# Decays of the SSD scan kept as exponentials in DRAM, with the cumulative sums and the long conv moved

## The chip, the cores and the metric

One core of a Trainium2 chip runs the whole program. The metric is the device time of one execution in microseconds. The core's engines run side by side, each from its own in-order queue: TensorE (PE, matrix products), VectorE (DVE), ScalarE (ACT), GpSimd (POOL) and SyncE (SP). They wait for one another by semaphores. DMAs are issued from the queues of SP, ACT and POOL.

## The reference, cut to what matters

One layer of a decoder trunk for 2048 prompt tokens and 8 x 8 sample tokens. After an RMS norm, one projection feeds three mixers (a Mamba-2 scan "SSD", a Conformer convolution, causal pooling), whose outputs are projected, gated and added.

```python
def trunk(x, states, start_pos, params):
    h = rmsnorm(x, norm_w)
    z, xbc, dt_raw, glu_in, gate_b, u_pool, gate_c, merge = split(h @ w_in)
    ya = mamba_branch(z, xbc, dt_raw, ...)     # conv of 4 taps, SSD scan, gated norm
    yb = conformer_branch(glu_in, gate_b, ...) # GLU, conv of 31 taps, layer norm
    yc = pool_branch(u_pool, gate_c, ...)
    ga, gb, gc = split(sigmoid(merge))
    x = x + (ga * (ya @ w_a) + gb * (yb @ w_b) + gc * (yc @ w_c)) @ w_out
    return rmsnorm(x, final_norm_w)

def ssd_scan(x, dt, a_log, b_mat, c_mat, h0):   # chunks of 128 tokens, 16 heads
    a_cum = cumsum(dt * A)                      # inside a chunk
    decay = exp(where(mask, a_cum[l] - a_cum[s], -inf))
    y_diag = (C_l . B_s) * decay @ (x * dt)
    states = B * exp(a_cum[last] - a_cum) * (x * dt)
    h = exp(a_cum[last]) * h + states           # chunk after chunk
    y_off = C * exp(a_cum) * h_enter
    return y_diag + y_off, h
```

## The kernel before, in words

All weights and activations of the large products are split into a high and a low float16 part; a block of a product takes 3 x 8 matmuls of 128 x 128 by up to 512 columns (`mm3`, L355). Tokens come in five blocks of 512, 512, 512, 256 and 320 columns (`TB`; `hT0` to `hT4` are the normed inputs). The order on PE is written by hand for the whole program; the order on DVE is written by hand in two stretches (`order.open()`), elsewhere a scheduler places the instructions of DVE, ACT, POOL and SP when the program is built. Weights come through a loader in steps: load, maximum on ACT (L227), a diagonal (L127), a PE product (L135) whose maximum DVE takes (L137, `prw`), powers of two on POOL (L157 to L241), the high part on ACT (L246), the low part on DVE (L250).

The stages that matter here, in order:

- GLU, second half: for each block four products (two of `glu_g`, two of `glu_v`; column pairs 2 and 3), evicted by a sigmoid on ACT (L446, tile `sg`) and a product on DVE (L455, tile `vt`). The PSUM tiles `mm` have three buffers. Before it, the time steps of the SSD heads are computed on DVE in a chain of small operations that ends with `dtA` (L611). After block 0 comes `cumulate` (L617 ff.): products of `dtA` with triangles and ones on PE (tile `dpt`, three buffers), copies `at` and `acum` and exponentials `etot`, `etos`, `dte` on ACT. The cumulative sums go to DRAM (`acT_d`, `acTs_d`), transposed. After blocks 1 to 3 `decay_early` loads and computes the decays of the first three scan units.
- DVE also runs the 31-tap convolution (`conv31`, L714; pieces of 1024 tokens, one accumulator `acc`, stored by POOL to `c_d`, L732): 68 steps ahead of the xbc stage, 1.9 per 512 columns inside it.
- xbc stage: 12 column blocks of products, evicted by ACT into `ue` (L766), convolved over 4 taps (`ct`, L780, L782), passed through SiLU to DRAM.
- Scan: a unit is a chunk `c` and a head group `g`, 17 x 2 units. Each loads `R` (cumulative sums broadcast over 128 partitions, 8 heads, 512 KB, L656) and `R2` (the same rows, broadcast over 64 partitions for each head of a pair, two DMAs of 128 KB, L662). ACT turns `R` into decays between tokens (8 Relus L672, one exponential L673) and `R2` into exp(a_cum) (L674). DVE forms `xd` (L871), `R` times `cbm` (L873) and, after PE's `off` products, `R2` times `off` (L899) plus `y` (L900); `R2` then leaves for `y_d` on POOL's queue (L903). `R` and `R2` have four buffers each. Between a unit's parts PE does the products of the pooling branch and a gate (`fillers`), at a pace set by `SR`; `pu` (L982) and `sgc` (L1032) are their evictions on ACT, `sw` (L1001) the pooling sums on DVE, `pus` (L987) a load of sample states. In each unit `conv_steps(CB)` is called twice.
- The sample pieces of the long conv (4 of them, 64 tokens) take seven steps each: products `pr` (L728) in four steps, reductions (L730) in two, and one more. The other pieces take 32 steps (31 operations of 512 columns and an empty one). `conv_steps(4)` is called for each of eight sample states at the scan's end, and `conv_steps(7)` for each unit of the merge.
- Merge of the first branch (`merge_units(0)`): gate product, projection, evictions on ACT (L1184) and DVE (L1189). Beside it run the rest of the long conv on DVE and the layer norm `ln_all`, which starts 12 us of the hand order's own clock after the merge does.
- Then the second branch, the gated norm of the scan's output, the third branch and the output product.

Of the kernel before, what the change touches and what calls it, by code (L numbers as in the profile page):

```python
# [10 lines left out]
F32 = mybir.dt.float32  # L11
# [3 lines left out]
AF = mybir.ActivationFunctionType  # L15
ALU = mybir.AluOpType
AX = mybir.AxisListType
# [3 lines left out]
P = 128  # L21
# [3 lines left out]
TS = 64  # L25
NB = 8
AHEAD = 2
TL = 8
T = TP + TS
H = 16  # L30
# [21 lines left out]
def trunk_body(tc, I, O):  # L52
# [16 lines left out]
    drp = pool("dram", 1, space=DRAM)  # L69
# [542 lines left out]
    acT_d = drp.tile([NC * H, P], F32, name="acT_d")  # L612
    acTs_d = drp.tile([H, TS], F32, name="acTs_d")

    def cumulate():

        def dpt(n):  # L617
            return dps.tile([P, 512], F32, name="dpt", tag="dpt", bufs=3)[:, :n]

        for i in range(2):  # L620
            pa = dpt(P)
            PE.matmul(pa, dtA[:, i * P:(i + 1) * P], tri, start=True, stop=True)
            at = tp.tile([P, P], F32, name="at", tag="at", bufs=2)
            S.activation(at, pa, AF.Copy)
            DMA.dma_start(out=acT_d[i * P:(i + 1) * P], in_=at)
        pa = dpt(TS)
        PE.matmul(pa[:H], dtA[:TS, NC * H:ND], tris, start=True, stop=True)
        at = tp.tile([P, P], F32, name="at", tag="at", bufs=2)
        S.activation(at[:H, :TS], pa[:H], AF.Copy)
        DMA.dma_start(out=acTs_d, in_=at[:H, :TS])  # L630
        pa = dpt(ND)
        PE.matmul(pa[:, :NC * H], tri, dtA[:, :NC * H], start=True, stop=True)
        PE.matmul(pa[:TS, NC * H:], tris, dtA[:TS, NC * H:ND], start=True, stop=True)
        S.activation(acum[:, :NC * H], pa[:, :NC * H], AF.Copy)
        S.activation(acum[:TS, NC * H:], pa[:TS, NC * H:], AF.Copy)
        pa = dpt(ND)
        PE.matmul(pa[:, :NC * H], ones, dtA[:, :NC * H], start=True, stop=True)
        PE.matmul(pa[:TS, NC * H:], blks, dtA[:TS, NC * H:ND], start=True, stop=True)
        S.activation(etot, pa[:, :NC * H], AF.Exp)
        V.tensor_tensor(dte[:, :NC * H], pa[:, :NC * H], acum[:, :NC * H], op=SUB)  # L640
        V.tensor_tensor(dte[:TS, NC * H:], pa[:TS, NC * H:], acum[:TS, NC * H:], op=SUB)
        S.activation(dte[:, :NC * H], dte[:, :NC * H], AF.Exp)
        S.activation(dte[:TS, NC * H:], dte[:TS, NC * H:], AF.Exp)

        dtm = tp.tile([P, NB, H], F32, name="dtm")
        V.tensor_tensor(dtm[:TS], dtA[:TS, NC * H:ND].unsqueeze(1).to_broadcast([TS, NB, H]),
                        ind.unsqueeze(2).to_broadcast([TS, NB, H]), op=MUL)
        pa = dpt(NB * H)
        PE.matmul(pa, ones[:TS], dtm[:TS].rearrange("p b h -> p (b h)"), start=True, stop=True)
        S.activation(etos, pa.rearrange("p (b h) -> p b h", h=H), AF.Exp)  # L650

    def decay_load(c, g):
        L = P if c < NC else TS
        R = dcp.tile([P, 8, P], F32, name="R", tag="R")[:, :, :L]
        rows = acT_d[c * H + 8 * g:c * H + 8 * g + 8] if c < NC else acTs_d[8 * g:8 * g + 8]
        DMA.dma_start(out=R[:L], in_=rows.unsqueeze(0).to_broadcast([L, 8, L]))  # L656

        def decays():

            R2 = dcp.tile([P, 4, P], F32, name="R2", tag="R2")[:, :, :L]  # L660
            for hh in range(2):
                DMA.dma_start(out=R2[hh * 64:(hh + 1) * 64],  # L662
                              in_=rows.rearrange("(b two) l -> two b l", two=2)[hh].unsqueeze(0).to_broadcast([64, 4, L]))
            return R2

        return R, decays

    def decay_exp(c, g, L, R, R2):

        for h in range(8):  # L670
            col = c * H + 8 * g + h
            S.activation(R[:L, h], R[:L, h], AF.Relu, scale=-1.0, bias=acum[:L, col:col + 1])  # L672
        S.activation(R[:L], R[:L], AF.Exp, scale=-1.0)  # L673
        S.activation(R2, R2, AF.Exp)  # L674


    early = {}
# [1 line left out]
    def decay_early(c, g):  # L679
        R, decays = decay_load(c, g)  # L680
        early[c, g] = R, decays()
        decay_exp(c, g, P, *early[c, g])

    for bi in range(5):
        for cb in (2, 3):
            glu_v(cb, (bi, 0, TB[bi][1]), wv2, iv2, glu_g(cb, (bi, 0, TB[bi][1]), wg2, ig2))
        if bi == 0:
            cumulate()
        elif bi < 4:
            decay_early(*((0, 0), (0, 1), (1, 0))[bi - 1])  # L690
    dps.release()
    tp.release()
    gp.release()
# [7 lines left out]
    def conv31(cp_, cb, t0, n, bufs):  # L701

        acc = cp_.tile([P, n], F32, name="acc", tag="acc", bufs=1)
        if t0 < TP:
            vt = cp_.tile([P, 30 + n], F32, name="vx", tag="vx", bufs=bufs)
            if t0 == 0:
                G.memset(vt[:, :30], 0.0)
                DMA.dma_start(out=vt[:, 30:], in_=v_d[cb, :, :n])
            else:
                DMA.dma_start(out=vt, in_=v_d[cb, :, t0 - 30:t0 + n])  # L710
            V.tensor_scalar(acc, vt[:, 30:], fw[:, cb, 30:31], fb[:, cb:cb + 1], op0=MUL, op1=ADD)
            for j in range(30):
                yield
                V.scalar_tensor_tensor(acc, vt[:, j:j + n], fw[:, cb, j:j + 1], acc, op0=MUL, op1=ADD)  # L714
        else:
            vt = cp_.tile([P, NB, TL + 30], F32, name="vs", tag="vx", bufs=bufs)
            DMA.dma_start(out=vt[:, :, :30], in_=I["st_cf"][cb])
            DMA.dma_start(out=vt[:, :, 30:], in_=v_d[cb, :, t0:t0 + n].rearrange("p (b t) -> p b t", t=TL))
            DMA.dma_start(out=O["cf_s"][cb], in_=vt[:, :, TL:])
            dst = acc.rearrange("p (b t) -> p b t", t=TL)  # L720
            w_ = fw[:, cb].unsqueeze(1).to_broadcast([P, NB, 31])
            for h in range(0, TL, 4):
                yield
                pr = ssp.tile([P, NB, 4, 31], F32, name="pr", tag="pr", bufs=1)
                for t in range(4):
                    if t == 2:
                        yield
                    V.tensor_tensor(pr[:, :, t], vt[:, :, h + t:h + t + 31], w_, op=MUL)  # L728
                yield
                V.tensor_reduce(dst[:, :, h:h + 4], pr, axis=AX.X, op=ADD)  # L730
            S.activation(acc, acc, AF.Identity, bias=fb[:, cb:cb + 1])
        G.dma_start(out=c_d[cb, :, t0:t0 + n], in_=acc)  # L732
        conv_done.append((cb, t0))
        yield
# [122 lines left out]
    def ssd_front(c, g, L, R, R2, xc):  # L857
# [4 lines left out]
            PE.transpose(px[:L, b * P:(b + 1) * P], xc[:, b], ident)  # L862
            yield
        if (c, g) not in early:
            decay_exp(c, g, L, R, R2)
        gs = slice(c * H + 8 * g, c * H + 8 * g + 8)
        return c, g, L, gs, R, R2, px, cbm

# [187 lines left out]
    fill = fillers()  # L1056
    SR = 1.7
    SI = 8
    CB = 0.3
    CC = 7.0  # L1060
    YP = (2.0, 3.0)
    SA, SC = 1, 4.0
# [190 lines left out]
            yield from ln_steps(bi)  # L1253
            yield LN_GAPS[3]

    side.add(ln_all(), 12.0)
    for _ in merge_units(0):
        conv_steps(CC)
        if not ybp and len(yc16) == len(TB):
# [314 lines left out]
```

## Time and profile before

| what | value |
|---|---|
| times of three runs | 2234.08, 2234.93, 2238.9 us (median 2234.93) |
| profiled execution | 2234.28 us, span 2232.5 us |
| mean granted clock | 0.987 |
| busy | PE 2124.0, PEld 1288.6, DVE 1369.1, ACT 913.6, POOL 256.5 us |
| moved by DMA | 259.57 MB |

The span runs from the first to the last instruction. Busy shares are over all stages, and the stages have different limits, so that the table by stage and the waits say more than the shares. "A <- B" in a wait means that an instruction of A stood ready in its queue until B had ended; times of waits of engines off the critical path cost nothing by themselves. The clock column is the granted clock of PE, as a share of 2.4 GHz.

### The profile page before, as it was taken

How to read it: one execution, taken by the hardware profiler on the slowest of the kernel's cores; microseconds unless marked ns; L12 is line 12 of the kernel's file. 1: busy time of each engine (PE TensorE's matmuls, PEld its weight loads, DVE VectorE, ACT ScalarE, POOL GpSimd, SP SyncE). 2: the span in 40 equal slices, each digit the busy share in tenths (PEclk: the TensorE clock that was granted, in tenths of full speed). 3: DMA queues.
4: the chain of work that ended last, by engine and by line, in shares of the span. 5: the costliest groups of instructions: out<-in, count | busy, mean ns of one | idle time of the engine just before them, and what ended most of it. 6: DMA issues, size and time to landing. Idle time of an engine off the chain costs nothing.

```text
span 2232.5 us, 33860 instructions
## 1 busy us (share of the span) xinstructions
PE 2124.0 (95%) x13188; PEld 1288.6 (58%) x13188; DVE 1369.1 (61%) x2413; ACT 913.6 (41%) x1651; POOL 256.5 (11%) x579
## 2 busy tenths in 40 slices
PE   5979999999889899999999999999999999999998
PEld 4544555555556566645545555556655555556887
DVE  6788679895667776878984344435676332332544
ACT  6535344444666567153423232224443232233322
POOL 0010011121110110132211011110000000000322
PEclk9998999999999999999999999999999999999999
DMA  6433222224565545552323233334341321227321
GB/s 242 142 91 116 62 86 78 78 86 158 164 151 161 164 141 172 168 170 90 96 93 104 75 110 113 106 106 128 111 137 40 103 93 47 85 91 237 105 100 53
DMA packets 203504, 259.57 MB, mean 116 GB/s; under 512 B 51408, under 2 KB 142160, under 8 KB 203344
## 3 DMA queue, kind: packets, MB, share of 16 engines
q1 hardware_dynamic: 184848, 218.89, 31.9%
q0 software_dynamic: 6896, 22.30, 2.8%
q10 hardware_dynamic: 11600, 16.22, 2.1%
q8 instruction: 103, 1.69, 0.3%
q14 instruction: 57, 0.47, 0.1%
HBM read 179.06 MB, written 78.30 MB: 115 GB/s over the span
## 4 chain that ended last, share of the span: by engine, by line
PE 60%; DVE 16%; issue 9%; DMA 8%; ACT 4%; POOL 2%; SPq 1%; POOLq 0%; DVEq 0%; ACTq 0%
PE mm L355 47%; DVE acc L714 7%; DVE ct L782 4%; PE po L1436 2%; PE po L1437 2%; PE po L1438 2%; DMA R<-acT_d 2%; DVE w L250 1%; DMA c_d<-acc 1%; DMA xs<-xbc_d 1%; DMA wst<-in_w_in 1%; DMA lc<-c_d 1%; ACT w L246 1%; PE gp L355 1%; PE y L887 1%
## 5 line engine op out<-in xcount | busy, mean ns | idle before, releaser
L355 PE MATMUL mm<-hT,w 128*128 128x512 f16 (+2 forms) x7728 | 1487.4, 342 | 25.9 <-ACT ue L766 6.7
L355 PEld LDWEIGHTS <-w 128*128 128x128 f16 x9696 | 951.2, 99 | 762.2 <-issue 84.1
L714 DVE SCALAR_TENSOR_TENSOR acc<-vx,vec,acc 128x512 f32<-128x512 f32 (+1 forms) x330 | 326.9, 991 | 6.1
L355 PE MATMUL mm<-ya,w 128*128 128x512 f16 (+2 forms) x888 | 161.9, 339 | 0.0
L246 ACT ACTIVATE w<-wst,sw 128x1024 f16<-128x1024 f32 x86 | 94.5, 1141 | 139.3 <-POOL sw L161 137.1
L1184 ACT ACTIVATE msg<-mm,winv 128x512 f32<-128x512 f32 (+2 forms) x80 | 48.6, 607 | 213.2 <-PE mm L355 204.5
L1189 DVE SCALAR_TENSOR_TENSOR msg<-mm,mi,msg 128x512 f32<-128x512 f32 (+2 forms) x80 | 52.3, 654 | 132.9 <-PE mm L355 110.3
L227 ACT ACTIVATE w<-wst 128x1024 f16<-128x1024 f32 x86 | 90.2, 1051 | 98.8 <-DMA wst<-in_w_in 64.1
L250 DVE SCALAR_TENSOR_TENSOR w<-wst,sw,w 128x1024 f16<-128x1024 f32 x86 | 107.1, 1280 | 36.6 <-ACT w L246 36.5
L1403 DVE SCALAR_TENSOR_TENSOR sg<-mm,winv,sg 128x512 f32<-128x512 f32 (+2 forms) x37 | 24.0, 649 | 157.4 <-PE mm L355 157.4
L782 DVE SCALAR_TENSOR_TENSOR ct<-ue,vec,ct 128x1024 f32<-128x1024 f32 (+1 forms) x108 | 101.6, 950 | 30.3 <-ACT ct L780 27.7
L157 POOL TENSOR_SCALAR pcw<-prw 128x1 f32<-128x1 f32 x49 | 21.2, 432 | 812.2 <-DVE prw L137 761.5
L1436 PE MATMUL po<-w,m 128*128 128x256 f16 x384 | 104.7, 273 | 0.0
L1438 PE MATMUL po<-w,m 128*128 128x256 f16 x384 | 104.7, 273 | 0.0
L1437 PE MATMUL po<-w,m 128*128 128x256 f16 x384 | 104.7, 273 | 0.0
L355 PE MATMUL mm<-yc,w 128*128 128x512 f16 (+2 forms) x480 | 96.4, 344 | 1.3 <-DVE yc L1142 1.2
L672 ACT ACTIVATE R<-R,acum 128x128 f32<-128x128 f32 (+1 forms) x272 | 82.6, 385 | 35.0 <-DMA R<-acT_d 27.4
L355 PE MATMUL mm<-yb,w 128*128 128x512 f16 (+2 forms) x480 | 92.8, 342 | 0.4 <-ACT msg L1184 0.4
L1449 DVE SCALAR_TENSOR_TENSOR xo<-po,winv,xo 128x256 f32<-128x256 f32 (+1 forms) x68 | 32.7, 483 | 72.0 <-PE po L1438 71.0
L1414 ACT ACTIVATE mt<-ml,msc 128x512 f16<-128x512 f32 (+2 forms) x35 | 22.6, 645 | 125.1 <-DVE ml L1404 117.1
L1451 ACT ACTIVATE jo<-xo 128x256 bf16<-128x256 f32 (+1 forms) x68 | 28.3, 416 | 100.6 <-DVE xo L1449 69.9
L1452 POOL TENSOR_TENSOR xo<-xo,fnw 128x256 f32<-128x256 f32 (+1 forms) x68 | 50.0, 737 | 151.0 <-ACT jo L1451 117.2
(293 smaller groups left out, 2407.0 us busy)
## 6 DMA issues: line engine op xcount, KB each, us to landing
wst<-in_w_in SPq DMA_DIRECT2D x64, 512.0 KB, 4.7
R<-acT_d SPq DMA_DIRECT2D x32, 512.0 KB, 4.7
xbc_d<-so SPq DMA_DIRECT2D x24, 512.0 KB, 2.6
m_d<-msg SPq DMA_DIRECT2D x48, 256.0 KB, 2.0
ml<-m_d SPq DMA_DIRECT2D x48, 256.0 KB, 2.8
R<-acT_d SPq DMA_DIRECT2D x64, 128.0 KB, 3.2
xc<-xbc_d SPq DMA_DIRECT2D x32, 256.0 KB, 3.3
y_d<-R POOLq DMA_DIRECT2D x32, 256.0 KB, 3.7
```

What stands on the lines that cost most here:

```text
L227: S.activation(w[:, 0, ks], st, AF.Abs, accum_out=mk)
L246: S.activation(w[:, 0, ks], st, AF.Copy, scale=s)
L250: V.scalar_tensor_tensor(w[:, 1, ks], st, s, w[:, 0, ks], op0=MUL, op1=SUB)
L355: PE.matmul(ps, w[:, i, k, c0:c0 + cw_], a[:, j, k, a0:a0 + n], start=(q == 0), stop=(q == len(passes) - 1))
L672: S.activation(R[:L, h], R[:L, h], AF.Relu, scale=-1.0, bias=acum[:L, col:col + 1])
L714: V.scalar_tensor_tensor(acc, vt[:, j:j + n], fw[:, cb, j:j + 1], acc, op0=MUL, op1=ADD)
L782: V.scalar_tensor_tensor(dst, src[j], cw[:, cb, j:j + 1], dst, op0=MUL, op1=ADD)
L1189: V.scalar_tensor_tensor(sg, po, iv, sg, op0=MUL, op1=MUL)
L1436: PE.matmul(ps, mh, wt[:, 0, k], start=(k == 0), stop=False)
L1437: PE.matmul(ps, mh, wt[:, 1, k], start=False, stop=False)
L1438: PE.matmul(ps, ml_, wt[:, 0, k], start=False, stop=(k == KD - 1))
L1452: G.tensor_tensor(xs, xs, fnw[:w, c * 256:(c + 1) * 256], op=MUL)
```

## The change

Beside `acT_d` and `acTs_d` the exponentials of the cumulative sums are kept in DRAM (`aeT_d`, `aeTs_d`), written by `cumulate` with three more activations and three more stores. `R2` is loaded from these, so that the exponential L674 goes. `R2` gets five buffers instead of four. `cumulate` is recorded after block 1 instead of block 0, and the three `decay_early` after blocks 2, 3 and 4. A step of a sample piece of the long conv is now two products and one reduction of half the size, five steps a piece. `CB` goes from 0.3 to 0.6, and the layer norm starts at 8 instead of 12.

```diff
+    aeT_d = drp.tile([NC * H, P], F32, name="aeT_d")
+    aeTs_d = drp.tile([H, TS], F32, name="aeTs_d")
     def cumulate():
...
+        ats = []
         for i in range(2):
...
-            at = tp.tile([P, P], F32, name="at", tag="at", bufs=2)
+            at = tp.tile([P, P], F32, name="at", tag="at", bufs=3)
             S.activation(at, pa, AF.Copy)
             DMA.dma_start(out=acT_d[i * P:(i + 1) * P], in_=at)
+            ats.append((at, P, aeT_d[i * P:(i + 1) * P]))
...
+        for at, n, to in ats:
+            r = H if n < P else P
+            ae = tp.tile([P, P], F32, name="ae", tag="ae", bufs=2)
+            S.activation(ae[:r, :n], at[:r, :n], AF.Exp)
+            DMA.dma_start(out=to, in_=ae[:r, :n])
...
-            R2 = dcp.tile([P, 4, P], F32, name="R2", tag="R2")[:, :, :L]
+            R2 = dcp.tile([P, 4, P], F32, name="R2", tag="R2", bufs=5)[:, :, :L]
+            erows = aeT_d[c * H + 8 * g:c * H + 8 * g + 8] if c < NC else aeTs_d[8 * g:8 * g + 8]
...
-    def decay_exp(c, g, L, R, R2):
+    def decay_exp(c, g, L, R):
...
         S.activation(R[:L], R[:L], AF.Exp, scale=-1.0)
-        S.activation(R2, R2, AF.Exp)
...
-        if bi == 0:
+        if bi == 1:
             cumulate()
-        elif bi < 4:
-            decay_early(*((0, 0), (0, 1), (1, 0))[bi - 1])
+        elif bi > 1:
+            decay_early(*((0, 0), (0, 1), (1, 0))[bi - 2])
...
-            for h in range(0, TL, 4):
+            for h in range(0, TL, 2):
                 yield
-                pr = ssp.tile([P, NB, 4, 31], F32, name="pr", tag="pr", bufs=1)
-                for t in range(4):
-                    if t == 2:
-                        yield
+                pr = ssp.tile([P, NB, 2, 31], F32, name="pr", tag="pr", bufs=1)
+                for t in range(2):
                     V.tensor_tensor(pr[:, :, t], vt[:, :, h + t:h + t + 31], w_, op=MUL)
-                yield
-                V.tensor_reduce(dst[:, :, h:h + 4], pr, axis=AX.X, op=ADD)
+                V.tensor_reduce(dst[:, :, h:h + 2], pr, axis=AX.X, op=ADD)
...
-    CB = 0.3
+    CB = 0.6
...
-    side.add(ln_all(), 12.0)
+    side.add(ln_all(), 8.0)
```

Three places show how instructions move. First PE, around the products of `cumulate` (`dpt`); `hT_77`, `hT_78` and `hT_79` are the inputs of blocks 0, 1 and 2, and the `w_` are the weights of the GLU's two halves. Before:

```order
L355 LDWEIGHTS w_1255
L355 MATMUL mm<-hT_77,w_1255 128x512
L622 MATMUL dpt<-cst,dtA 128x128 x2
L627 MATMUL dpt<-cst,dtA 16x64
L632 MATMUL dpt<-dtA,cst 128x256
L633 MATMUL dpt<-dtA,cst 64x16
L637 MATMUL dpt<-dtA,cst 128x256
L638 MATMUL dpt<-dtA,cst 64x16
L649 MATMUL dpt<-dtm,cst 128x128
L355 LDWEIGHTS w_654
L355 MATMUL mm<-hT_78,w_654 128x512
```

Now:

```order
L355 LDWEIGHTS w_1255
L355 MATMUL mm<-hT_78,w_1255 128x512
L626 MATMUL dpt<-cst,dtA 128x128 x2
L632 MATMUL dpt<-cst,dtA 16x64
L638 MATMUL dpt<-dtA,cst 128x256
L639 MATMUL dpt<-dtA,cst 64x16
L643 MATMUL dpt<-dtA,cst 128x256
L644 MATMUL dpt<-dtA,cst 64x16
L655 MATMUL dpt<-dtm,cst 128x128
L355 LDWEIGHTS w_654
L355 MATMUL mm<-hT_79,w_654 128x512
```

The eight products stand between blocks 1 and 2 instead of between blocks 0 and 1; nothing else moves on PE there.

Second ACT at the same place. `w_1910` before and `w_1879` now are the same weight block, `at`, `acum`, `etot`, `etos` and `dte` the tiles of `cumulate`. Before:

```order
L246 ACTIVATE w_1735<-wst,sw 128x1024 x2
L227 ACTIVATE w_1910,wm_1981<-wst 128x1024
L227 ACTIVATE w_1910,wm_1983<-wst 128x1024
L229 ACTIVATE wm_1983<-wm_1983,wm_1981 128x1
L127 ACTIVATE dgm<-cst,wm_1983 128x128
L624 ACTIVATE at<-dpt 128x128 x2
L629 ACTIVATE at<-dpt 16x64
L634 ACTIVATE acum<-dpt 128x256
L635 ACTIVATE acum<-dpt 64x16
L639 ACT_TABLE_LOAD
L639 ACTIVATE etot<-dpt 128x256
L650 ACTIVATE etos<-dpt 128x128
```

Now:

```order
L127 ACTIVATE dgm<-cst,wm_1952 128x128
L446 ACTIVATE sg<-mm,winv 128x512
L246 ACTIVATE w_1879<-wst,sw 128x1024 x2
L628 ACTIVATE at<-dpt 128x128 x2
L634 ACTIVATE at<-dpt 16x64
L660 ACT_TABLE_LOAD
L660 ACTIVATE ae<-at 128x128 x2
L640 ACTIVATE acum<-dpt 128x256
L641 ACTIVATE acum<-dpt 64x16
L645 ACTIVATE etot<-dpt 128x256
L656 ACTIVATE etos<-dpt 128x128
L660 ACTIVATE ae<-at 16x64
```

The two conversions L246 of the weight block, which stood far behind `cumulate`, now stand ahead of its first copy, and the exponentials `ae` behind the copies.

Third ACT in the scan, at the end of the second pooling group; `R_6013` is an `R2`, L1032 and now L1040 the sigmoid-gate eviction `sgc`. Before:

```order
L229 ACTIVATE wm_6261<-wm_6261,wm_6259 128x1
L127 ACTIVATE dgm<-cst,wm_6261 128x128
L674 ACTIVATE R_6013<-R_6013 128x512
L1032 ACT_TABLE_LOAD
L1032 ACTIVATE sgc<-mm,winv 128x320
L672 ACTIVATE R<-R,acum 128x128 x8
L673 ACT_TABLE_LOAD
```

Now:

```order
L229 ACTIVATE wm_6307<-wm_6307,wm_6305 128x1
L127 ACTIVATE dgm<-cst,wm_6307 128x128
L1040 ACT_TABLE_LOAD
L1040 ACTIVATE sgc<-mm,winv 128x320
L684 ACTIVATE R<-R,acum 128x128 x8
L685 ACT_TABLE_LOAD
```

The exponential of `R2` (L674) is gone from between the two; it goes in the same way in all units.

## Rows read from the trace of the kernel before

**Rows 1.** The page, busy us (share of the span) and instructions of each engine.

```profile
PE 2124.0 (95%) x13188; PEld 1288.6 (58%) x13188; DVE 1369.1 (61%) x2413; ACT 913.6 (41%) x1651; POOL 256.5 (11%) x579
```

**Rows 2.** Stages; columns: stage, us, busy us (count) by engine, granted clock, DMA.

```profile
155.06:169.22 14.16, 0.00 (x1) 0.03 (x1) 14.16 (x19) 4.78 (x7) 4.58 (x5) 0.62 0.26 93
169.22:178.90 9.68, 9.68 (x27) 4.74 (x28) 6.75 (x8) 6.91 (x22) 0.90 (x2) 0.50 0.55 160
...
241.00:506.00 265.00, 258.69 (x1452) 141.63 (x1450) 221.92 (x210) 120.47 (x189) 38.75 (x67) 1.00 0.24 79
...
540.00:890.00 350.00, 321.88 (x2168) 213.91 (x2167) 236.53 (x377) 232.26 (x459) 41.43 (x85) 0.98 0.55 159
...
958.00:1180.00 222.00, 205.90 (x1150) 114.19 (x1148) 191.79 (x316) 90.28 (x124) 49.89 (x108) 0.98 0.32 103
```

**Rows 3.** Timeline of PE around `cumulate`: start, us, operation, count, [idle before <-releaser].

```profile
134.10 18.52 PE L355 MATMUL mm<-hT,w 128*128 128x512 f16 x85
...
169.22 1.19 PE L622 MATMUL dpt<-cst,dtA 128*128 128x128 f32 x4 [14.17 <-issue]
...
170.66 1.22 PE L632 MATMUL dpt<-dtA,cst 128*128 128x256 f32 x2
...
174.33 21.27 PE L355 MATMUL mm<-hT,w 128*128 128x512 f16 x87
195.44 0.22 PE L135 MATMUL mm<-dgm,ones 128*128 128x128 bf16 x1
```

**Rows 4.** Timeline of DVE, same stretch.

```profile
156.50 0.28 DVE L137 TENSOR_REDUCE prw<-mm 128x1 f32<-128x128 f32 x1
...
168.68 0.43 DVE L611 SCALAR_TENSOR_TENSOR dtA<-dt__1677,ea 128x272 f32<-128x272 f32 x1
...
170.44 3.91 DVE L714 SCALAR_TENSOR_TENSOR acc<-vx,vec,acc 128x1024 f32<-128x1024 f32 x3
...
183.73 0.81 DVE L711 TENSOR_SCALAR acc<-vx,vec 128x1024 f32<-128x1024 f32 x1 [7.62 <-DMA c_d<-acc]
```

**Rows 5.** Timeline of ACT, same stretch.

```profile
159.00 2.19 ACT L246 ACTIVATE w<-wst,sw 128x1024 f16<-128x1024 f32 x2 [8.46 <-POOL sw L161]
```

**Rows 6.** Groups of the scan: xcount | busy us, mean ns | idle before.

```profile
L674 ACT ACTIVATE R<-R 128x512 f32<-128x512 f32 x28 | 17.6, 627 | 38.4 <-DMA R<-acT_d 37.1 <-DVE sw L1014 1.2
...
L728 DVE TENSOR_TENSOR pr<-vs,vec 128x248 f32<-128x248 f32 x24 | 8.8, 408 | 0.0
...
L730 DVE TENSOR_REDUCE acc<-pr 128x32 f32<-128x992 f32 x5 | 5.9, 1177 | 0.0
```

**Rows 7.** Waits of ACT in the scan: us in total, times, longest.

```profile
ACT R L674 <- DMA R<-acT_d: 37.1, 12, 7.2
ACT R L672 <- DMA R<-acT_d: 26.6, 15, 9.0
ACT L674 <- DMA R<-acT_d: 14.3, 4, 7.0
```

**Rows 8.** Waits of SP's DMA queue in the scan.

```profile
SPq L662 <- DMA y_d<-R: 110.1, 28, 9.1
...
SPq L987 <- DMA out_pool_s<-pus: 24.8, 3, 10.3
```

**Rows 9.** Timeline of the scan, one row of ACT and one of PE.

```profile
655.43 0.63 ACT L674 ACTIVATE R<-R 128x512 f32<-128x512 f32 x1 [7.18 <-DMA R<-acT_d]
...
668.86 1.97 PE L887 MATMUL y<-R,xd 128*64 128x128 f32 x16 [4.47 <-DVE R L900]
```

**Rows 10.** PE in the scan: two rows of its timeline, one of its waits.

```profile
606.64 1.12 PE L905 MATMUL st<-xe,bt 128*128 128x512 f32 x2 [1.86 <-DVE state L910]
...
796.53 1.68 PE L887 MATMUL y<-R,xd 128*64 128x128 f32 x16 [3.92 <-DVE R L900]
...
PE y L887 <- DVE R L900: 15.4, 6, 4.5
```

**Rows 11.** Group of the merge stage (958 to 1180).

```profile
L714 DVE SCALAR_TENSOR_TENSOR acc<-vx,vec,acc 128x512 f32<-128x512 f32 x150 | 112.2, 748 | 2.0
```

More of the change, by code (lines that the diff above doesn't have):

```diff
@@ L622, in cumulate @@
             PE.matmul(pa, dtA[:, i * P:(i + 1) * P], tri, start=True, stop=True)
-            at = tp.tile([P, P], F32, name="at", tag="at", bufs=2)
+            at = tp.tile([P, P], F32, name="at", tag="at", bufs=3)
             S.activation(at, pa, AF.Copy)
             DMA.dma_start(out=acT_d[i * P:(i + 1) * P], in_=at)
+            ats.append((at, P, aeT_d[i * P:(i + 1) * P]))
         pa = dpt(TS)
         PE.matmul(pa[:H], dtA[:TS, NC * H:ND], tris, start=True, stop=True)
-        at = tp.tile([P, P], F32, name="at", tag="at", bufs=2)
+        at = tp.tile([P, P], F32, name="at", tag="at", bufs=3)
         S.activation(at[:H, :TS], pa[:H], AF.Copy)
         DMA.dma_start(out=acTs_d, in_=at[:H, :TS])
+        ats.append((at, TS, aeTs_d))
         pa = dpt(ND)
@@ L658, in decays @@
         def decays():
-            R2 = dcp.tile([P, 4, P], F32, name="R2", tag="R2")[:, :, :L]
+            R2 = dcp.tile([P, 4, P], F32, name="R2", tag="R2", bufs=5)[:, :, :L]
+            erows = aeT_d[c * H + 8 * g:c * H + 8 * g + 8] if c < NC else aeTs_d[8 * g:8 * g + 8]
             for hh in range(2):
                 DMA.dma_start(out=R2[hh * 64:(hh + 1) * 64],
-                              in_=rows.rearrange("(b two) l -> two b l", two=2)[hh].unsqueeze(0).to_broadcast([64, 4, L]))
+                              in_=erows.rearrange("(b two) l -> two b l", two=2)[hh].unsqueeze(0).to_broadcast([64, 4, L]))
             return R2
         return R, decays
-    def decay_exp(c, g, L, R, R2):
+    def decay_exp(c, g, L, R):
         for h in range(8):
@@ L681, in decay_early @@
         early[c, g] = R, decays()
-        decay_exp(c, g, P, *early[c, g])
+        decay_exp(c, g, P, R)
     for bi in range(5):
@@ L864, in ssd_front @@
         if (c, g) not in early:
-            decay_exp(c, g, L, R, R2)
+            decay_exp(c, g, L, R)
         gs = slice(c * H + 8 * g, c * H + 8 * g + 8)
```

## The prediction

> **What bounds the kernel now.** I read the page's busy line first, then the table by stage, then TensorE's waits, and last the timelines of ACT, DVE and SP around the longest waits. PE is busy 95% of the span and the next engine 61% [rows 1], so only time in which PE waits or runs at its lower clock can be won. The table by stage shows where that is [rows 2]: PE does nothing for 14.2 us in front of the products of `cumulate` and then has 9.7 us at a granted clock of 0.50 (1.2 GHz); it is idle 350.00 - 321.88 = 28.1 us in the scan (540 to 890), 222.00 - 205.90 = 16.1 us in the merge of the first branch (958 to 1180), and 6.3 us of 265 in the xbc stage. The diff touches all four. The remaining stages stay as they are.
>
> **Part 1: `cumulate` a token block later.** In before PE ends block 0 at 155.05 and waits until 169.22 [rows 3], because `dtA` comes off DVE at 168.68 + 0.43 = 169.1 [rows 4]. In the new order block 1 is multiplied first. It costs what block 0 cost, 155.05 - 134.10 = 20.96 us, so PE reaches `cumulate` at 176.0, 6.9 us after `dtA`. That wait is gone. What is late next stands in the order of ACT: the copies `at` now stand behind the two weight conversions of L246. These wait for a maximum on DVE, and that for a PE product 87/96 into block 1, at 174.1. On DVE the maximum comes behind five more convolution steps of 3.91 / 3 = 1.30 us and two small operations (0.9 us, estimated) after `dtA` [rows 4]: 169.1 + 6.5 + 0.9 + 0.3 = 176.8. From the end of such a maximum (156.50 + 0.28) to L246 took 2.2 us and L246 itself 2.19 [rows 4, 5], so `at` is copied at 179.0 + 2.2 + 0.3 (the copy, estimated) = 181.5. There are three `dpt` buffers, so the fourth product waits for it: PE idles some 4.6 us from 176.9. After the fourth product 174.33 - 170.66 = 3.7 us are left, which was at half clock [rows 3]; I keep that figure. Block 2 then starts at 185.2. In before it starts nine products after 195.44, at 197.4 [rows 3]. Gain 12.2 us. From this I take 2 us for the first two sigmoids of block 2: the exponentials of `dte` now stand in ACT's queue ahead of them and wait for DVE, which first waits for the store of the finished convolution piece (a wait that was 7.62 us [rows 4]) and its three PSUM buffers just about cover it. **Part 1: -10 us.** Bounds: -18.8 if nothing waits at `at` (197.4 less 176.0 and 2.6, the 5.1 us of the eight products [rows 3] at full clock), -5 if DVE is as late again as the 4.6 us.
>
> The added copies to DRAM (three exponentials, three small stores) come after `at` and are read by loads that nothing needs before the scan; cost 0, at most the 2 us above once more. The xbc stage starts 10 us earlier with the same DVE backlog in front of it. DVE has 265.00 - 221.92 = 43 us to spare in it [rows 2], so I take 0, with +6 as the bound (PE's waits there double).
>
> **Part 2: the decays R2 come as exponentials, with a fifth buffer.** Removed are 28 `R2` exponentials in the scan, 17.6 us of ACT [rows 6], and two more of the sample chunk. Worth more than their time is what they wait for: ACT sits 37.1 + 14.3 = 51.4 us in front of them for the R2 load [rows 7], with PSUM evictions queued behind. The load in turn is late because SP waits 28 times, 110.1 us, for the `y_d` store out of the buffer that it refills [rows 8]: with four buffers that is the store of the unit just finished, with five the one before it, which has landed. One such chain in full: at 655.43 ACT has waited 7.18 us for R2, its sigmoid and the eviction of `pu` come late, DVE with them, and at 668.86 PE has stood 4.47 us for the DVE operation that frees `y` [rows 9]. Afterwards R2 is needed only by DVE's L899, three units after its load. I went through the waits of PE in the scan one by one: of 28.1 us seven, the first 1.86 us at 606.64 and the last 3.92 us at 796.53, follow such an ACT wait [rows 10]; with the five between they make 18.1 us. The other 10, two of them also between, follow loads that SP issues late for another reason (24.8 us for `pus` [rows 8]) or DVE, and stay. The granted clock was 0.98 over the stage, 7 us of the 350 at full speed [rows 2], a part of them idle anyhow; I take 4 us.
>
> **Part 3: the long conv at twice the pace in the scan (CB 0.3 to 0.6, finer sample steps).** 34 units now take 40.8 steps where they took 20.4. In before these were all sample steps, 8.8 + 5.9 = 14.7 us of DVE [rows 6]. After, all four sample pieces (32 products of 0.408 us = 13.1; 16 half reductions between 0.6 and 1.18 us each, say 0.66, = 10.6) and 20.8 convolution steps of 0.75 us [rows 11] (15.6) come to 39 us, 24 more. DVE is idle 350 - 236.5 = 113.5 us there [rows 2], most of it waiting for ACT, so they fit, but each step stands ahead of `xd` and the R product on DVE's queue. I charge 4 us for it. **Scan: -18.1 - 4 + 4 = -18 us.** Bounds: -30 (all idle time and the clock) and +24 (every added microsecond lands on PE).
>
> In return 28 steps of 0.75 us (20.4 + 32 of 28 + 192 are done when the merge starts, then 40.8 + 32 of 20 + 192) leave the merge: 21 of DVE's 191.8 us in 222 [rows 2]. PE's 16.1 us of waits are waits for DVE. The pace per merge unit stays at 7, so the first units are as crowded as before and only the last four are relieved: I take 5 us, a third. Bounds 0 and -16. The layer norm starting 4 us of its own clock earlier moves a handful of products and costs nothing by itself.
>
> **Sum.** The profiled execution took 2234.28 us (span 2232.5), 0.65 under the median of 2234.93, so sum and median can be compared directly. 2234.3 - 10 - 18 - 5 = **2201 us**.
>
> **A rule that speaks against it.** The waits show relief on ACT as worth more than its time [rows 7 to 9]. The Trainium skill, page "Perfetto Trace Analysis", section "Identifying the Most-Contended Engine", says the opposite way of choosing: find the engine with the highest occupancy and optimize this one first. By that rule, taking work from ACT (41%) and bringing it nearer on DVE (61%) leaves the scan at its length, and the sum would be rival A's below. This trace bears it out only as far as PE is the bound: 28.1 us of PE's idle time have ACT or DVE at the end.
>
> **The rivals.**
> A. The scan keeps its length: other waits end last in the same places. For it: ACT waits for R as well (26.6 us), and SP's stop for `pus` [rows 8] holds back R and xc loads in the new order as before; against it: in the chain at 655 to 669 the R2 load alone was late [rows 9]. Time 2234.3 - 10 - 5 = 2219. Chance 0.13.
> B. More than I take: `at` isn't late, and DVE's relief in the merge counts twofold. 2234.3 - 17 - 24 - 8 = 2185. For it: the two weight conversions are one DVE operation away from being early; against: their order is fixed. Chance 0.17.
> C. Slower: the conv steps on DVE. Each stands in front of `xd`, the R product, and the L899/L900 that free PSUM for PE's next `y`; if DVE's spare time per unit (113.5 / 34 = 3.3 us) isn't where the step falls, PE waits for the whole of it: +24 in the scan, nothing won there. 2234.3 - 10 - 5 + 24 = 2243. It decides from the point where the step (two products and a reduction, 1.4 us) is longer than the lead of L900 over the next `y`. For it: 15.4 us of PE's waits are already for L900 [rows 10]; against it: these follow ACT's stops. Chance 0.06.
> D. The change does not move the time: part 1's wait comes back in the xbc stage (+6, and the waits for the sigmoids), and A holds. 2232. Chance 0.03.
>
> **How the numbers follow.** My forecast has 0.61; its own range is 2191 to 2212. The range for 8 in 10 takes in A and B: 2184 to 2220. What a measurement can tell from no change is 0.2%, 4.5 us. Faster: 0.61 + 0.13 + 0.17 = 0.91; same: D and a little of A and C, 0.04; slower: 0.05.
>
> **What would show it.** Right: no wait of 14 us before `cumulate`, but one of 3 to 6 us inside it, for ACT; block 2 started by 184 to 188; no ACT wait for R2, no SP wait of R2 for `y_d`, R2 waits on DVE near zero; PE idle in the scan near 10 us, in the merge near 11. Wrong: PE's waits for L900 or `xd` grow in the scan (C), ACT's waits for R grow to what R2's were (A), or PE's waits for `ue` in the xbc stage reach 12 us.

## The result and the profile after

The changed kernel takes 2205.15 us (median of four, 2201.87 to 2210.85), beside 2236.1 us for the kernel before on the same chip: a ratio of 0.9863, interval 0.9838 to 0.9889, 31 us less. The profiled execution took 2201.87 us with a span of 2200.1, 32.4 less than before. Line numbers are 4 to 12 higher than before, in the scan mostly 8 (L657 to L661 are the new exponentials and their stores); `R2`'s loads are now L674, its L899/L900 are L907/L908, and `y_d` is stored in L911.

The stages of after, cut at the same PE instructions as before (by their count), so that each row stands against one of before; columns as in [rows 2]:

```profile
132.08:227.93 95.85, 92.95 (x499) 49.87 (x496) 85.88 (x93) 44.84 (x86) 6.90 (x13) 0.95 0.33 104
227.93:492.04 264.11, 260.09 (x1453) 142.03 (x1451) 227.34 (x214) 120.84 (x188) 43.58 (x69) 0.99 0.26 83
492.04:526.01 33.97, 33.30 (x164) 17.00 (x162) 17.32 (x24) 14.86 (x28) 2.68 (x10) 1.00 0.52 163
526.01:864.88 338.87, 320.61 (x2168) 212.40 (x2167) 256.06 (x417) 212.80 (x427) 41.85 (x87) 0.97 0.56 165
864.88:932.88 68.00, 68.00 (x400) 41.12 (x399) 54.11 (x79) 11.14 (x17) 8.80 (x17) 1.00 0.52 182
932.88:1148.43 215.55, 203.83 (x1151) 114.21 (x1149) 171.67 (x285) 91.05 (x124) 46.99 (x107) 0.99 0.32 105
```

The rows are GLU with `cumulate`, xbc, the scan's lead-in, scan, samples and merge. Before they lasted 107.0, 265.0, 34.0, 350.0, 68.0 and 222.0 us. The gain is 11.2 in the first, 11.1 in the scan, 6.4 in the merge and 0.9 in xbc; 1.9 more lies before 132 and 0.8 after the merge, where nothing was changed (other runs of the same code up to 132 gave 131.3 to 134.0, so that this is scatter).

`cumulate` first, PE and ACT in after (start, us, operation, idle before and what ended it), against [rows 3, 5]:

```profile
153.80 19.80 PE L355 MATMUL mm<-hT,w 128*128 128x512 f16 x91
...
175.44 0.61 PE L626 MATMUL dpt<-cst,dtA 128*128 128x128 f32 x4
175.98 0.28 PE L632 MATMUL dpt<-cst,dtA 64*16 64x64 f32 x2
179.16 0.70 PE L638 MATMUL dpt<-dtA,cst 128*128 128x256 f32 x2 [2.90 <-ACT at L628]
...
182.01 10.21 PE L355 MATMUL mm<-hT,w 128*128 128x512 f16 x35
```

```profile
176.76 2.19 ACT L246 ACTIVATE w<-wst,sw 128x1024 f16<-128x1024 f32 x2 [5.67 <-POOL sw L161]
178.86 0.42 ACT L628 ACTIVATE at<-dpt 128x128 f32<-128x128 f32 x2
```

The wait of 14.17 us is gone, and the new one stands where it was expected: inside `cumulate`, for a copy that ACT makes only after the two weight conversions L246.

In the scan, what ACT, SP, DVE and PE waited for (us in total, times, longest), against [rows 7, 8, 10] and, for DVE, one row of before, which is shown ahead of the one of after:

```profile
ACT R L684 <- DMA R<-acT_d: 83.5, 24, 10.6
```

```profile
SPq L674 <- DMA y_d<-R: 86.4, 24, 8.3
...
SPq L995 <- DMA out_pool_s<-pus: 24.9, 3, 12.8
```

```profile
DVE sw L1001 <- ACT pu L982: 59.3, 16, 5.8
```

```profile
DVE sw L1009 <- ACT pu L990: 33.4, 10, 7.9
```

```profile
PE tr L870 <- ACT acc L739: 8.0, 1, 8.0
...
PE y L895 <- DVE R L908: 1.2, 2, 1.0
```

PE's idle time in the scan fell from 28.1 to 338.87 - 320.61 = 18.3 us. Its waits for L900 (now L908), 15.4 us before, are down to 1.2. But one stop, 3.46 us before, is now 7.95 us (8.0 in the row), ACT waits for loads as long as before (83.5 us where it was 37.1 + 26.6 + 14.3 = 78.0), and SP still stands in front of R2 for `y_d`. The following rows of after, DVE first, then SP and ACT, show where the 8 us come from:

```profile
572.79 0.69 DVE L1009 TENSOR_TENSOR sw<-pu 128x514 f32<-128x514 f32 x1 [7.89 <-ACT pu L990]
...
575.07 0.73 DVE L737 TENSOR_TENSOR pr<-vs,vec 128x248 f32<-128x248 f32 x2
575.84 0.67 DVE L738 TENSOR_REDUCE acc<-pr 128x16 f32<-128x496 f32 x1
576.42 0.41 DVE L861 TENSOR_TENSOR cbm<-tr,cst 128x256 f32<-128x256 f32 x1
```

```profile
558.83 0.59 SPq L995 DMA_DIRECT2D pus<-in_st_pool  x1
559.52 0.61 SPq L834 DMA_DIRECT2D xc<-xbc_d  x1
560.23 1.25 SPq L674 DMA_DIRECT2D R<-aeT_d  x2
561.57 0.55 SPq L667 DMA_DIRECT2D R<-acT_d  x1
```

```profile
567.38 2.44 ACT L684 ACTIVATE R<-R,acum 128x128 f32<-128x128 f32 x8 [10.62 <-DMA R<-acT_d]
...
572.09 0.67 ACT L990 ACTIVATE pu<-mm,winv 128x512 f32<-128x512 f32 x1
```

An R load is issued late (561.57), ACT stops 10.62 us for it with the eviction of `pu` behind it, DVE stops 7.89 us for `pu`, and `cbm`, which frees the `tr` tile that PE wants, stands on DVE behind the pooling sums and a step of the long conv (1.4 us, which did not stand there before). PE goes on at 576.94, 0.11 us after `cbm` ends. (The profile names L739 as the releaser, which ends at nearly the same time; at the same place before, PE went on 0.10 us after `cbm` with no L739 about.)

### The profile page after: what moved, and what is told of

It is laid out like the page before. It is cut to its first block, busy times and chain, and to the rows that moved or that the text cites. A ratio compares the mean times of both kernels' runs of the same rounds, so it can differ in the third digit from the quotient of the medians.

```text
span 2200.1 us, 33800 instructions
## 1 busy us (share of the span) xinstructions
PE 2119.2 (96%) x13188; PEld 1286.1 (58%) x13188; DVE 1370.0 (62%) x2421; ACT 895.8 (41%) x1618; POOL 254.9 (12%) x579
## 4 chain that ended last, share of the span: by engine, by line
PE 68%; DVE 15%; DMA 6%; issue 4%; ACT 3%; POOL 2%; SPq 0%; POOLq 0%; DVEq 0%; ACTq 0%
PE mm L355 52%; DVE acc L725 7%; DVE ct L790 3%; PE po L1444 3%; PE po L1445 3%; PE po L1446 2%; DVE w L250 1%; DMA R<-acT_d 1%; PE y L895 1%; DMA c_d<-acc 1%; DMA xs<-xbc_d 1%; DMA wst<-in_w_in 1%; PE st L913 1%; PE off L905 1%; ACT w L246 1%
## 5 line engine op out<-in xcount | busy, mean ns | idle before, releaser
L246 ACT ACTIVATE w<-wst,sw 128x1024 f16<-128x1024 f32 x86 | 94.5, 1141 | 138.6 <-POOL sw L161 138.0
L250 DVE SCALAR_TENSOR_TENSOR w<-wst,sw,w 128x1024 f16<-128x1024 f32 x86 | 107.2, 1280 | 40.9 <-ACT w L246 40.9
L227 ACT ACTIVATE w<-wst 128x1024 f16<-128x1024 f32 x86 | 90.3, 1051 | 96.7 <-DMA wst<-in_w_in 62.6
L790 DVE SCALAR_TENSOR_TENSOR ct<-ue,vec,ct 128x1024 f32<-128x1024 f32 (+1 forms) x108 | 101.7, 950 | 19.2 <-ACT ct L788 16.6
```

Source lines behind the costliest of these rows:

```text
L227: S.activation(w[:, 0, ks], st, AF.Abs, accum_out=mk)
L246: S.activation(w[:, 0, ks], st, AF.Copy, scale=s)
L250: V.scalar_tensor_tensor(w[:, 1, ks], st, s, w[:, 0, ks], op0=MUL, op1=SUB)
L790: V.scalar_tensor_tensor(dst, src[j], cw[:, cb, j:j + 1], dst, op0=MUL, op1=ADD)
```

## The experiments

Stage lengths are from one profiled execution of each, cut at the same PE instructions, in us. That execution lay between 7.0 us under (b_pace) and 4.3 us over (b_cum) the median of its kernel, so a few us of one stage say little by themselves. The ratio is of medians, to before on the same chip:

| run | GLU, cumulate | xbc | scan (PE idle) | merge | ratio to before (interval) |
|---|---|---|---|---|---|
| before | 107.0 | 265.0 | 350.0 (28.1) | 222.0 | |
| after | 95.9 | 264.1 | 338.9 (18.3) | 215.6 | 0.9863 (0.9838-0.9889) |
| b_cum | 96.4 | 266.8 | 352.3 (27.1) | 222.1 | 0.9957 (0.9945-0.9969) |
| b_exp4 | 109.3 | 265.7 | 340.3 (21.7) | 222.4 | 0.9963 (0.9951-0.9974) |
| b_exp4_busy | 112.5 | 267.3 | 337.3 (19.2) | 221.9 | 0.9987 (0.9972-1.0002) |
| b_buf5 | 106.9 | 264.0 | 353.9 (32.1) | 221.9 | 1.0026 (1.0016-1.0035) |
| b_step | 107.2 | 265.1 | 356.2 (34.6) | 223.4 | 1.0030 (1.0017-1.0044) |
| b_cb | 106.8 | 265.0 | 350.3 (30.4) | 219.1 | 1.0016 (1.0003-1.0030) |
| b_pace | 106.9 | 264.8 | 342.0 (20.7) | 215.4 | 0.9975 (0.9962-0.9988) |
| a_buf4 | 96.7 | 264.1 | 337.0 (19.2) | 215.0 | 0.9867 (0.9841-0.9893) |
| a_cb3 | 95.6 | 262.8 | 333.7 (16.1) | 218.8 | 0.9879 (0.9853-0.9905) |
| a4_pus2 | 93.6 | 263.7 | 338.2 (17.6) | 214.5 | 0.9870 (0.9845-0.9895) |
| a4_pusP | 96.1 | 264.5 | 342.0 (21.4) | 215.5 | 0.9894 (0.9863-0.9925) |
| a4_pusP_r2P | 96.2 | 263.3 | 330.5 (11.9) | 214.8 | 0.9831 (0.9800-0.9861) |

Runs named b_ change the kernel before, runs named a_ the changed kernel.

**b_cum: the place of `cumulate` alone.**

```diff
-        if bi == 0:
+        if bi == 1:
             cumulate()
```

> The kernel before with the place of `cumulate` alone changed (after block 1, decay_early after blocks 2 to 4). Theory (the wait in front of the products goes and is not paid back): PE's wait of 14.2 us becomes 3 to 5 us inside `cumulate` for ACT's copies, the xbc stage starts 10 to 12 us earlier, the time falls by 10 to 13 us, to a ratio of 0.994 to 0.9955. Rival (the wait comes back in the xbc stage, where DVE's convolution is the same amount late): `ue` waits there grow to over 10 us and the ratio is 0.998 to 1.000.

The stage is 10.6 us shorter, xbc 1.8 longer, the time 9.8 us or 0.43% less, just under the theory's range. PE waits 4.17 us inside `cumulate` for `at`, and its waits for `ue` in the xbc stage are 7.5 us (6.3 before). The theory stands; most of the wait isn't paid back.

**b_exp4: the exponentials alone, four buffers.**

```diff
+            erows = aeT_d[c * H + 8 * g:c * H + 8 * g + 8] if c < NC else aeTs_d[8 * g:8 * g + 8]
...
-        S.activation(R2, R2, AF.Exp)
```

> The kernel before with the exponentials in DRAM alone, R2 with its four buffers as before. Theory (what counts is that ACT has nothing left to wait for in R2): PE's idle time in the scan falls from 28 to 10 to 16 us and the time by 10 to 18 us, ratio 0.992 to 0.9955, although SP still waits some 110 us for the store out of the buffer. Rival 1 (the fifth buffer is what brings the load in time): without it the R loads queued on SP behind R2's wait come as late, ACT's waits for R grow by what R2's fall, idle time in the scan stays at 24 us or more and the ratio is 0.998 to 1.002. Rival 2 (ACT's busy time of 17.6 us is what is given back): about 18 us of it, which can't be told from the theory by this run alone.

The scan is 9.7 us shorter, the time 0.37% less: most of the scan's gain needs no fifth buffer. The PE idle time is above what the theory had (21.7 against 10 to 16), and the ratio lies between the theory's range and rival 1's. ACT's stops went from R2 to R, as rival 1 had it: for R it waits 76.2 us (26.6 before), so that its waits for loads are in all as long as before (78.0). What got shorter is DVE's wait for `pu`, 59.3 us before:

```profile
ACT R L684 <- DMA R<-acT_d: 76.2, 22, 7.6
```

```profile
DVE sw L1012 <- ACT pu L993: 44.1, 13, 9.0
```

The chain that the prediction tells in full [rows 9] is still there: ACT stops 7.59 us for R where it stopped 7.18 for R2, and PE stands 4.95 us at the same place (4.47 before, 4.46 in b_exp4_busy).

```profile
659.52 2.44 ACT L684 ACTIVATE R<-R,acum 128x128 f32<-128x128 f32 x8 [7.59 <-DMA R<-acT_d]
```

```profile
670.08 1.98 PE L898 MATMUL y<-R,xd 128*64 128x128 f32 x16 [4.95 <-DVE R L911]
```

And 2.3 us are lost before xbc, where PE waits for a sigmoid of the GLU:

```profile
198.69 5.56 PE L355 MATMUL mm<-hT,w 128*128 128x512 f16 x25 [2.27 <-ACT sg L446]
```

**b_exp4_busy: the same, with ACT's time put back but not its wait.**

```diff
         S.activation(R[:L], R[:L], AF.Exp, scale=-1.0)
+        S.activation(R[:L, :4], R[:L, :4], AF.Copy)
```

> The kernel before with the exponentials in DRAM and four buffers (it shortened the scan from 350 to 340.3 us), plus, after the exponential of R in each unit, an in-place copy on ACT of 128 x 512 elements of R: as long as the exponential that was removed (627 ns, 28 in the scan and 4 beside it) but with no load to wait for. Theory (the wait for the R2 load was the price): the scan stays at 339 to 344 us, ratio 0.995 to 0.998. Rival (ACT's busy time was the price): the scan is back at 347 us or more, ratio 0.998 to 1.001.

The scan's group of the added copy (count, busy us, mean ns, idle before):

```profile
L686 ACT ACTIVATE R<-R 128x512 f32<-128x512 f32 (+1 forms) x30 | 18.4, 612 | 0.5
```

The copies put 18.4 us back (ACT is busy 227.4 us in the scan; 232.3 before, 211.0 in b_exp4; some 5 us of table loads stay away), and the scan is still short, 337.3 us, below even the theory's range. So the time that ACT worked there was worth nothing to PE. What is left as the price is ACT's stop for R2; how far the runs together show that stands in the next section, under the scan. The total came out above the theory's range, in the rival's (0.9987), for reasons outside the scan: three of the copies stand in ACT's queue ahead of a sigmoid of the GLU (at 198.36) that PE waits for, 3.97 us at 199.10, and the GLU stage is 5.5 us longer than before. xbc is 2.3 longer, though PE's waits for `ue` are as before (6.1 us, 6.3 before); the granted clock was 0.50 for 6.8 us from 422.1, at the end of a stop of 3.43 us, and 1.00 all through the stage before.

**b_buf5 and b_step: the fifth buffer with the exponential kept, and the finer sample steps that make its room.**

```diff
-            R2 = dcp.tile([P, 4, P], F32, name="R2", tag="R2")[:, :, :L]
+            R2 = dcp.tile([P, 4, P], F32, name="R2", tag="R2", bufs=5)[:, :, :L]
```

> The kernel before with a fifth buffer for R2, the exponential on ACT kept; the sample pieces of the long conv in the finer steps, whose smaller `pr` makes the room, at the old pace. Theory (ACT's wait for R2 is the price): the buffer brings the load a unit earlier, ACT's 51 us of waits for R2 fall below 15, and the time falls by 8 to 15 us, ratio 0.993 to 0.9965. Rival (SP is only let one unit further ahead and still stands for the store, so that R and xc loads behind it come no earlier): ACT waits for R instead, idle time in the scan stays at 22 us or more, ratio 0.998 to 1.002.

> The kernel before with the sample pieces in five finer steps alone, pace 0.3 kept. The pace part shortened the scan by 8 us though it put 20 us more of DVE's work into it. Theory 1 (the longest steps are what delays the y path: a step of 1.18 us becomes one of 0.66, behind two products): this run has the gain, the scan 5 to 8 us shorter, ratio 0.996 to 0.998. Theory 2 (the order of DVE's queue changes with the pace, by where the steps fall): the scan within 3 us of before, or longer, ratio 0.999 to 1.002.

Both are slower by some 0.3%, b_step by the steps alone as much as b_buf5 with the buffer: the buffer gave nothing. ACT's waits for R2 hardly changed (32.5 + 14.9 us, before 37.1 + 14.3), and its waits for R rose to 37.2. The theory of b_buf5 falls.

**b_cb and b_pace: the pace alone, and with finer steps and the layer norm at 8.**

```diff
-    CB = 0.3
+    CB = 0.6
```

> The kernel before with the pace alone at 0.6, the old sample steps, layer norm at 12. Theory 1 (finer steps make the gain in the scan): the scan 0 to 8 us longer, the merge 4 to 6 us shorter, ratio 0.998 to 1.001. Theory 2 (it is the pace that moves other instructions on DVE and ACT): the scan 5 to 8 us shorter and the merge 4 to 6, ratio 0.994 to 0.996.

> The kernel before with the pace alone: CB 0.6, sample pieces in five steps, layer norm at 8. Theory (the prediction's part 3): the scan is 0 to 4 us longer for 24 us more of DVE work in it, the merge 5 to 7 us shorter, together -6 to +1 us, ratio 0.997 to 1.0005. Rival (each conv step lands on PE): the scan 10 to 24 us longer, ratio 1.002 to 1.008.

The merge gains 2.9 us from the pace and 6.6 from all three. In the scan neither the steps (+6.2) nor the pace (+0.3) gains anything alone, and with both, and the layer norm at 8, it is 8.0 us shorter: theory 1 of b_step and theory 2 of b_cb, which give the gain to one part, both fall, and so does b_pace's for the scan, while its merge and ratio came as it had them. Part of the 8.0 may be scatter: the stages of b_pace's profiled execution give 14.6 us, the medians 6.2. What changes is how long PE waits for L900: 7.1 us in b_pace and 23.4 in b_step (before 15.4), with ACT's stops for R2 still there. Which instruction decides it stays open.

**a_buf4: after with four R2 buffers.**

> The changed kernel with four buffers for R2 instead of five. Theory 1 (the fifth buffer gives part of the scan's gain, as the prediction has it): the scan (338.9 us in the changed kernel) grows by 5 us or more, the time is 2209 us or more. Theory 2, formed after the runs of the single parts (with the exponential gone from ACT the fifth buffer only lets SP's queue run a unit further ahead and stand there for a store, with the R and xc loads behind it): the scan is as long or up to 8 us shorter, the stall of 8 us at the first `pus` load falls to 3 to 6 us, the time is 2195 to 2203 us.

The scan is 337.0 us, the time 2201.49 (ratio 0.9867, with the fifth buffer 0.9863): the fifth buffer does nothing here either, and theory 2 holds but for the stall, which stays (8.8 us). SP shows why. In after the R2 loads go out at 560.23 and 570.81, in a_buf4 at 561.33 and 572.40, with the stores of `y_d` at the same distances: with five buffers each load is put one unit earlier in SP's order (ten R2 DMAs are out before the scan's first store of `y_d`, in a_buf4 eight), and waits for a store that has just been issued, as before.

**a4_pus2 and a4_pusP: SP's stop for `pus`.** Both have four R2 buffers; a4_pus2 gives `pus` a second buffer, and the edit of a4_pusP is this:

```diff
-                DMA.dma_start(out=us[:, :, :15], in_=I["st_pool"][g])
+                G.dma_start(out=us[:, :, :15], in_=I["st_pool"][g])
```

> The changed kernel with four buffers for R2 and two instead of one for `pus` (736 bytes of a partition in the room of the fifth R2 buffer). Theory (the 8 us stall of the scan hangs on SP's queue, which stands 12.8 us for the store out of the only `pus` tile, with xc, R2 and R loads behind it): the stall goes at the first group, the scan is 6 to 9 us shorter than in the changed kernel with four buffers or at most 1 us longer than that, the time is 2190 to 2197 us. Rival (the R load is late for the y_d store anyway): ACT's wait for R there stays above 7 us, the stall keeps 4 us or more and the time is that of the four-buffer kernel within 2 us.

> The changed kernel with four R2 buffers and the load of the sample states into `pus` issued from POOL's queue instead of SP's. A second `pus` buffer did not take SP's stop away: the load was placed a group earlier and waited 12.2 us at the same place. Theory (that stop on SP, with xc, R2 and R loads behind it, makes PE's stall of 7 to 9 us near 575): SP has no such wait, ACT's wait of some 10 us for R there falls below 5, the stall falls to 0 to 3 us, the scan is 5 to 9 us shorter than 337 to 338 us, the time 2192 to 2197 us. Rival (the wst loads of 1 MB and the y_d stores at the same place make the R load late whoever issues pus): ACT's wait stays above 7 us, scan 335 to 339 us, time 2199 to 2203 us.

With a second `pus` buffer SP stands as long at the same place (12.2 us), for the load is put a group earlier; the stall is 6.9 us and the time that of a_buf4 (2201.54), as the rival had it. Issued on POOL's queue it no longer holds SP, and the stall is 8.65 us all the same: the theory falls, and the scan (342.0 us) is longer than the rival had it too. In a4_pusP the R load goes out at 562.55, behind an R2 load that waits for `y_d`, in the place where `pus` had stood:

```profile
561.22 1.25 SPq L674 DMA_DIRECT2D R<-aeT_d  x2
562.55 0.55 SPq L667 DMA_DIRECT2D R<-acT_d  x1
```

SP's waits for `y_d` rise to 122.3 us in it (96.7 in a_buf4).

**a4_pusP_r2P: the R2 loads on POOL's queue as well.**

```diff
-                DMA.dma_start(out=R2[hh * 64:(hh + 1) * 64],
+                G.dma_start(out=R2[hh * 64:(hh + 1) * 64],
...
```

> As the kernel before this one in the call, and the R2 loads issued from POOL's queue too, where the y_d stores they wait for are issued. Theory (SP's 86 to 105 us of waits for y_d hold back the R and xc loads and with them ACT's Relus): ACT's waits for R fall from some 80 us to below 30, PE's idle time in the scan to below 9 us, scan 325 to 331 us, time 2186 to 2194 us. Rival 1 (ACT's waits for R are off the path of PE by now): the scan within 2 us of the kernel without it. Rival 2 (POOL stands for the stores and holds back y_d, c_d and the weight loader's scales): scan or merge longer by 3 us or more.

2190.69 us, against 2207.53 for a4_pusP and 2201.58 for a_cb3 on the same chip, and 0.9831 of before, the lowest ratio of all. The scan is 11.5 us shorter than in a4_pusP, PE idles 11.9 us in it and the stall is 3.06. Against a_buf4, which has neither move, the scan is 6.5 shorter; the R2 loads were not moved alone. ACT's waits for R are only down to 60.8 us, so that part of the expectation was missed. The wait for the store now stands on the queue that issues the store, and R and xc loads pass it:

```profile
POOL R L674 <- DMA y_d<-R: 89.4, 26, 6.4
```

**a_cb3: after at the old pace.**

> The changed kernel with CB at 0.3 again (the finer sample steps and the layer norm at 8 stay). Theory (with ACT's stops for R2 gone a step on DVE costs PE nothing in the scan, and the pace is worth only what it takes from the merge): the scan 336 to 341 us as in the changed kernel, the merge 220 to 223 instead of 215.6, time 2206 to 2212 us. Rival (the pace also shortens the scan, as it did with the finer steps alone): the scan 344 us or more, time 2213 or more.

The merge is 218.8 us, 3.2 longer than in after; the scan is 333.7, 5.2 shorter. Theory and rival both miss the scan: in these two profiles the pace costs the scan more than it takes from the merge. The time, 2201.58 us (0.9879), can't be told from that of after.

## Why the prediction was right, point by point

**The total.** Forecast 2201 (0.985 of the median it was made against), measured 2205.15 on a chip where before took 2236.1 (0.9863). Right, within its own range, and in part by luck: the scan's term is 6.9 us too large, while the other stages gave 3.5 more than their terms and 2.7 of the profiled gain lies where nothing was changed.

**Part 1, -10: right in mechanism, and in size by errors that offset one another.** 11.2 us in after, 10.6 in b_cum. The steps hold: ACT's copies behind L246, the fourth product waiting. The wait was 2.90 us instead of 4.6, since PE reached `cumulate` 1.3 us later than one block of 20.96 had it (start-up differences taken out), and ACT's copy was half a microsecond earlier. After the wait the eight products' remainder took 2.85 us (3.7 forecast), but the clock was low for longer than I had it:

```profile
175.40:182.00 6.60, 3.70 (x17) 2.11 (x16) 3.94 (x4) 4.99 (x11) 1.46 (x7) 0.87 0.72 226
182.00:192.20 10.20, 10.20 (x37) 4.16 (x37) 9.99 (x11) 6.59 (x19) 0.00 (x0) 0.75 0.81 239
```

The first 10.2 us of block 2 had a mean of 0.75, part at 1.2 and part at 2.4 GHz, which costs some 2.5 us (an estimate: a quarter of 10.2). The 2 us for the sigmoids are not there as a wait of PE in after.

**xbc, 0: right** (-0.9; +1.8 in b_cum).

**The scan, -18: too much; measured -11.1.** The term had -14.1 us of PE's idle time (-18.1, and +4 for the conv steps) and -4 for the clock. The idle time fell by 9.8. PE's busy time fell by 1.3 (321.88 to 320.61) and the granted clock was 0.97 where it was 0.98, so 2.7 of the 6.9 us that are missing are the clock's term. In the idle time the step that failed is the fifth buffer's, that R2's load would then wait for "the one before it, which has landed": the extra buffer let the load be issued a unit earlier and wait for a fresher store, SP's queue was not relieved, and ACT's stops moved from R2 to R (26.6 to 83.5 us).

Of the seven waits of PE that I let go [rows 10], 18.1 us, 15.8 went; the first, at 606.64, stayed (2.20 us). The other 10 us, which I let stay, became 16.0. PE's stop of 3.46 us, where R2 load, `pus` and R load meet, grew to 7.95, of which 1.4 is the conv step ahead of `cbm`; and a stop of 2.77 us at 702 is new. The former also followed an ACT stop for R2 in before, and ACT now stops there for R:

```profile
578.42 1.28 ACT L674 ACT_TABLE_LOAD   x1 [6.96 <-DMA R<-acT_d]
```

The sign I had set for this, "no SP wait of R2 for `y_d`", came out wrong (86.4 us), and rival A's, "ACT's waits for R grow to what R2's were", came true without rival A's result.

That the exponential's removal shortens the scan is shown by the runs together rather than by one pair, for edits that leave ACT's work alone moved the scan by +6.2 (b_step) and -8.0 us (b_pace). The six kernels with the exponential have scans of 342.0 to 356.2 us, the eight without 330.5 to 342.0. That ACT's work was not the price is shown by b_exp4_busy. That its stop for R2 was, and how the stop reaches PE, is only in part shown: ACT waits for loads as long as before, but DVE waits less for `pu`. That wait is 55.0 to 59.3 us in the five kernels whose scan is 350 us or longer and 30.1 to 44.1 in the nine others, b_pace with the exponential kept among them (37.6). And the chain told in full [rows 9] did not go with the exponential (b_exp4); it went only in after and the kernels made from it (0.0 to 1.1 us), and which of their edits did it is open.

The +4 for DVE's added conv steps is not confirmed. After and a_cb3 differ by 5.2 us, but the same change of pace made +0.3 (before to b_cb) and -14.2 (b_step to b_pace, which also has the layer norm at 8). Rival C's +24 is in none of them.

**The merge, -5: right** (-6.4), of which the pace is 3.2 (a_cb3). The other 3.2 us are there with the pace set back, in a_cb3; b_step shows none of it, so the earlier layer norm, for which I took nothing, is the likely source. It was not run alone.

**The rule set against it.** The Trainium skill, page "Perfetto Trace Analysis", section "Identifying the Most-Contended Engine", says to optimize the engine with the highest occupancy first. That the scan would then keep its length was the prediction's own step: the sentence ranks engines and gives no time, and by busy time PE is first [rows 1], whose idle time the change went for. The runs show that an engine's share of busy time did not price relief on it here: an exponential taken off ACT, at 41%, with DVE's work unchanged, gave 9.7 us of the scan, and copies that put 18.4 us of work back took none of them away.

## What to carry to other kernels

On an engine that serves others from an in-order queue, look at what stands behind a waiting instruction, and not only at how long the engine works: 18 us of copies on ACT cost the scan nothing, where taking out an instruction that waited gave 10. When a wait goes, look at the queue that caused it: as long as the loads stand in one queue with a load that waits for a store, the wait turns up at the next load, and neither a fifth R2 nor a second `pus` buffer helped, since each was spent on issuing the load earlier. With the `pus` and R2 loads on the queue of the store that R2 waits for, the scan was shortest, 330.5 us. And price an edit by more than one pair of runs where small shifts move an order of in-order queues: the same change of pace was worth +5.2, +0.3 and -14.2 us of the scan in three kernels.

## What was not expected of the hardware

A store landed late with large loads queued beside it. In after the stores of `y_d` take 3.9 us to land in the median of the scan's first 160 us; between 550 and 572, with two loads `wst` of 512 KB issued from 562.22 on, the view has (KB each, median us to landing):

```profile
wst<-in_w_in SPq DMA_DIRECT2D x2, 512.0 KB, 8.0
y_d<-R POOLq DMA_DIRECT2D x2, 256.0 KB, 7.1
...
bc<-xbc_d SPq DMA_DIRECT2D x1, 256.0 KB, 8.9
```

The store issued at 562.74 landed 8.0 us later, and the R2 load behind it went out at 570.81; the other of the two, issued at 553.94 before those loads, took 6.2. At the same place the store took 8.2 us in before, 8.4 in a_buf4 and 8.4 in a4_pusP_r2P; three later stores of after beside `wst` loads took 2.9 to 5.2, so that size and place of the delay vary. And a stop of PE of 2.90 us was followed by 10.2 us at a mean granted clock of 0.75, some 2.5 us by the estimate above: here a short stop cost nearly its own length again. It need not: after a stop of 3.01 us at 1605 in the same trace the granted clock stayed at 1.00.
